# A SwiGLU chunk's silu, gate product and split, emitted in three pieces over three items

## The chip, the cores and the metric

The kernel runs on one core of one Trainium2 chip. The metric is the device time of one execution in microseconds, the lower the better. Engines are named as in the profile: PE (matmuls), PEld (weight loads into PE), DVE (elementwise on tensors), ACT (activations), POOL (small elementwise work and some DMA issues), SP (the queue that issues the weight loads from memory).

## The reference

A trunk of two layers on a sequence of 256 rows and width 1024. Each layer is a half-step SwiGLU, a token mixer (a gated causal mixing beside a sparse attention), and a second half-step SwiGLU. Each has an RMS norm ahead of it and a shift, a scale and a gate that come from a conditioning vector `c` by a matrix `ada_w` per layer.

```python
def swiglu(h, w_in, w_out):
    g, u = jnp.split(h @ w_in, 2, axis=-1)
    return (jax.nn.silu(g) * u) @ w_out

for l in range(DEPTH):
    mod = c_act @ ada_w[l] + ada_b[l]
    sh1, sc1, g1, sh2, sc2, g2, sh3, sc3, g3 = jnp.split(mod, N_MOD, axis=-1)
    h = modulate(rms_norm(x, norm_ffn1[l]), sh1, sc1)
    x = x + 0.5 * g1[:, None, :] * swiglu(h, ffn1_w_in[l], ffn1_w_out[l])
    ...
```

`w_in` is 1024 x 5632 and `w_out` 2816 x 1024, all float32.

## The kernel before

**Three products per product.** Every float32 operand of a matmul is split into a high part (rounded to the fast float32 form) and a low part (the rest). A matmul then is three: high by high, high by low, low by high. So a unit of weights, 512 KB loaded from memory into one of 7 buffers `raw` (`NRAW`), is split before use: ACT copies it to `whi` (L502), DVE subtracts to `wlo` (L507). The pair of `raw` readers, ACT and DVE, frees the buffer, and only then SP issues the next load into it. There are 10 pairs of `whi` and `wlo` (`NB`).

**The conditioning vectors ride along.** Rows of `ada_w` come through the same 7 buffers, woven between the units of weights. DVE multiplies and adds them into `aacc` (L489; the first of eight on ACT, L484). After the eighth, DVE folds the sum (L386), PE multiplies the folded sum by a small matrix (L399 or L431), and DVE finishes it (L402, or L435 and what follows). For the vectors named G the result goes out and back by two small DMAs that POOL issues (L395 fetches `ada_b`, L404 and L406 store and broadcast).

**The phases.** There are six: SwiGLU, mixer and SwiGLU for each layer, numbered 0 to 5. In a SwiGLU phase the 2816 columns are cut into chunks, chunk 0 of 512 columns, chunk 1 of 256, chunks 2 to 5 of 512. In phase 0, chunks 0 and 1 are part of a start-up; in phases 2, 3 and 5 chunk 0 is computed per half of the rows. All others are *joint chunks* (`joint_chunk`): both halves of the rows together, 8 items of one unit of weights each (4 items for chunk 1). A joint chunk takes as many of the 8 PSUM banks as it has blocks of 128 columns, four, or two for chunk 1. A bank holds 256 values of g and 256 of u. An item is 24 matmuls (L719), ordered by bank, so that a chunk's first bank is complete before its last.

After the last item the *gate* of each bank follows: ACT writes silu of g into the scratch tile `xm` (L741), DVE multiplies by u (L742), and the bank is given back. After each pair of banks comes the *split* of the result: ACT writes `aThi` (L536), DVE writes `aTlo` (L537). These are operands of the second product, `project`, which runs over 22 units of `w_out`, first ahead on one half of the rows by up to 7 items (`LAG`), then alternating between halves; an item there is 6 matmuls (L540 to L542).

**What sets the order.** Each engine works through its instructions in the order in which this code emits them, and waits at an instruction until its operands are there. After each item, `item_done` runs what was put off with `defer(n, ...)`, that is n items earlier, and then `pump` emits splits of weights and additions of `ada_w` rows: at most 2 units after an item of a joint chunk, 1 after others, and only while fewer than 8 units lie ahead. In phase 0 the code also emits steps of the rotary tables (`rope_tables`, L163 to L208): POOL does most of them, DVE casts in between (L178, L180, L202), and ACT takes the sines at the end (L198, L200, L206, L208).

Of the kernel before, what the change touches and what calls it, by code (L numbers as in the profile page):

```python
# [25 lines left out]
LAG = 6  # L26
NRAW = 7
HOLD = (3, 7)
TAIL = 3
VX = 188  # L30
FOLD_D = (2, 2, 4)
# [68 lines left out]
def trunk(ctx, tc, x_in, c_in, pos_in, ada_w, ada_b, norm_ffn1, ffn1_w_in, ffn1_w_out,  # L100
# [12 lines left out]
    bankp = ctx.enter_context(tc.tile_pool(name="bankp", bufs=1, space=bass.MemoryType.PSUM))  # L113
    banks = [bankp.tile([P, 512], F32, name=f"bank{i}") for i in range(8)]

    def take():
        return banks.pop(0)

    def give(*ts):
        banks.extend(ts)  # L120
# [206 lines left out]
    def defer(n, fn):  # L327
        pend.append([n, fn])
# [115 lines left out]
    late = []  # L444

    def pump_lo(n=1 << 20):
        while late and n > 0:
            e, hi, lo, r = late.pop(0)
            c = e["kt"] * e["cols"]
            V.tensor_tensor(lo[:, :c], e["raw"][:, :c], hi[:, :c].bitcast(F32), op=ALU.subtract)  # L450
            e["hi"], e["lo"], e["slot"] = hi, lo, r
            W.append(e)
            n_rd[0] += 1
            n -= 1
        dma_fill()
# [61 lines left out]
    def next_w(b):  # L517
        while wcur[b] >= len(W):
            if late:
                pump_lo(1)  # L520
            else:
                pump(1, force=True)
        e = W[wcur[b]]
        wcur[b] += 1
        kt, cols = e["kt"], e["cols"]
        n = kt * cols
        return (e["hi"][:, :n].rearrange("p (k c) -> p k c", k=kt),
                e["lo"][:, :n].rearrange("p (k c) -> p k c", k=kt), e["slot"])

    def release(b, w):  # L530
        if b == 1:
            ring[w[2]] = True


    def split_T(ps, hi, lo):
        S.activation(hi, ps, AF.Copy)  # L536
        V.tensor_tensor(lo, ps, hi.bitcast(F32), op=ALU.subtract)  # L537

    def mm3(ps, ahi, alo, whi, wlo, first, last):
        T.matmul(ps, ahi, whi, start=first, stop=False)  # L540
        T.matmul(ps, ahi, wlo, start=False, stop=False)  # L541
        T.matmul(ps, alo, whi, start=False, stop=last)  # L542
# [54 lines left out]
    def after_sub(b, pi):  # L597
        if pi + 1 < len(phases):
# [3 lines left out]
            pump_lo(1)  # L602
            hold[0] = HOLD[b]

# [22 lines left out]
    def project(b, pi, n, operand, hook):  # L627
        _, l, i, _ = phases[pi]
        final = pi + 1 == len(phases)
        parts = PARTS if final and b == 1 else HALF  # L630
        bk = [take() for _ in parts]
        acc = [t[:, :sl.stop - sl.start] for t, sl in zip(bk, parts)]

        def part(k, w, h):
            ahi, alo = operand(k)
            mm3(acc[h], ahi, alo, w[0][:, 0, parts[h]], w[1][:, 0, parts[h]], k == 0, k == n - 1)
        for k in range(n - TAIL):
            w = next_w(b)
# [4 lines left out]
            yield  # L643
        ws = [next_w(b) for _ in range(TAIL)]
        for h, sl in enumerate(parts):
            for i_ in range(TAIL):
                part(n - TAIL + i_, ws[i_], h)
                if h + 1 == len(parts):
                    release(b, ws[i_])
                if i_ == 1 and h == 0:  # L650
                    hook(n - TAIL)
                    yield
            if h < 2:
                hook(n - TAIL + h + 1)
            if not final and h != b:
# [17 lines left out]
    def ffn_gen(b, pi, env):  # L673
        hi, lo = hT(1, b)
        f = 0
        for c0, w in chunks[:1] if pi else ():
            kt = 1024 // w
            acc = [take() for _ in range(2)]
            for k0 in range(0, KD, kt):
                for s in range(2):  # L680
# [30 lines left out]
    def joint_chunk(env, ch, late=False):  # L711
        c0, w = chunks[ch]
        f, nj = c0 // P, w // P
        acc = [take() for _ in range(nj)]

        def mms(parts, pick):
            for o, col, wk, k, first in parts:
                for i_, (stat, mov) in enumerate(pick):
                    T.matmul(o, wk[stat][col], mov[:, :, k, :], start=first and i_ == 0 and mov is hThi  # L719
                             and stat == 0, stop=False, skip_group_check=True)  # L720

        for k0 in range(0, KD, 2):
            for ss in ((0,), (1,)) if w == 512 else ((0, 1),):
                w_ = next_w(0)
                wcur[1] = wcur[0]
                release(1, w_)
                parts = [(acc[j][:, s * 256:(s + 1) * 256],
                          (slice(None), kk, slice((0 if w == 512 else s * 256) + j * P,
                                                  (0 if w == 512 else s * 256) + j * P + P)),
                          w_, k0 + kk, k0 + kk == 0 and s == ss[0] and s == 0)  # L730
                         for j in range(nj) for kk in range(2) for s in ss]
                if late:
                    for p_ in ((0, hThi), (1, hThi), (0, hTlo)):
                        mms(parts, (p_,))
                else:
                    mms(parts, ((0, hThi), (0, hTlo), (1, hThi)))
                if k0 + 2 == KD and ss[-1] == 1:
                    scr = xm[0] if w == 512 else xm[1]
                    for j in range(nj):
                        a = scr[:, j * 256:(j + 1) * 256]  # L740
                        S.activation(a, acc[j][:, :256], AF.Silu)  # L741
                        V.tensor_tensor(a, a, acc[j][:, 256:], op=ALU.mult)  # L742
                        give(acc[j])
                        if j % 2:
                            def fin(j=j):
                                a2 = scr[:, (j - 1) * 256:(j + 1) * 256].rearrange(
                                    "p (f b t) -> p f b t", f=2, b=2)
                                split_T(a2, env["aThi"][:, f + j - 1:f + j + 1],
                                        env["aTlo"][:, f + j - 1:f + j + 1])
                            if late:  # L750
                                env.setdefault("todo", []).append(fin)
                            else:
                                fin()
                yield

    def joint_gen(env, first):
        for ch in range(first, len(chunks)):
            left = 8 if chunks[ch][1] == 512 else 4
            for _ in joint_chunk(env, ch):
                left -= 1  # L760
                yield left if first == 2 and ch + 1 < len(chunks) else 0
# [432 lines left out]
    def start(env):  # L1194
# [33 lines left out]
        load_cols(1)  # L1228
        load_small()
        ga, gb = joint_chunk(env, 0, True), joint_chunk(env, 1, True)  # L1230
        for g in range(NG):
            more = g + 1 < NG
# [41 lines left out]
    for pi, (kind, l, i, n) in enumerate(phases):  # L1274
        with ExitStack() as es:
            env = {}
# [87 lines left out]
```

## Time and profile before

| what | value |
|---|---|
| median of 3 runs | 996.51 us (995.94 to 996.64) |
| the profiled execution, its own time | 997.6 us |
| its span, first to last instruction | 995.9 us |
| PE busy | 971.5 us, 98% |
| DVE busy | 771.4 us, 77% |
| ACT busy | 531.4 us, 53% |
| POOL busy | 52.3 us, 5% |
| silu L741, 76 instructions | 26.1 us |
| gate product L742, 76 instructions | 29.4 us |
| split on ACT L536 and DVE L537 from `xm`, 38 each | 23.9 us and 26.2 us |
| matmuls L719 of the joint chunks, 3648 | 970.7 us, overlapping |

The time lies 1.7 us above the span, and the profiled execution 1.1 us above the median. Matmuls overlap in the records, so their busy times sum to more than they cover; the rate is read from the distance between starts. Times within the profile count from the span's start.

### The profile page before, as it was taken

To read this page: it belongs to the slowest core of one execution; us is meant where nothing else is said; L and a number is where in the kernel's file an instruction comes from. 1 tells how busy PE (TensorE), PEld (TensorE's weight loads), DVE (VectorE), ACT (ScalarE), POOL (GpSimd) and SP (SyncE) were. 2 spreads that over 40 slices of the span, in tenths; PEclk is the share of its full clock that TensorE was granted. 3 is DMA by queue.
4 is the path that set the end of the run, shared out by engine and by line. 5 is a ranking of instruction groups with operands and counts; after the bars stand their busy time and mean duration, and the time that the engine had idled before them with its cause. 6 is when DMAs were issued, how large, how long until landed. Compare 5 with 4: busy or idle time off the path is not lost.

```text
span 995.9 us, 16619 instructions
## 1 busy us (share of the span) xinstructions
PE 971.5 (98%) x6396; PEld 867.9 (87%) x6396; DVE 771.4 (77%) x1072; ACT 531.4 (53%) x794; POOL 52.3 (5%) x92
## 2 busy tenths in 40 slices
PE   7999997999999999999999999999999999999997
PEld 6899995887787899998888999988878789999886
DVE  6888998778997878886587788866889786766444
ACT  6464554356577755544355455435657776444331
POOL 4012400000000000000000000000000000000000
PEclk9999998999999999999999999999999999999999
DMA  9989998967665589888858888996766556766531
GB/s 334 386 279 335 332 348 342 352 225 239 193 190 151 172 293 336 319 320 311 278 180 297 301 311 304 338 309 183 224 197 191 151 172 215 250 241 231 178 134 43
DMA packets 110416, 253.47 MB, mean 255 GB/s; under 512 B 9138, under 2 KB 27620, under 8 KB 110336
## 3 DMA queue, kind: packets, MB, share of 16 engines
q1 hardware_dynamic: 108256, 248.06, 72.4%
q0 software_dynamic: 1792, 3.82, 1.2%
q8 instruction: 50, 0.82, 0.3%
q10 hardware_dynamic: 288, 0.52, 0.1%
q14 instruction: 30, 0.25, 0.1%
HBM read 251.30 MB, written 1.07 MB: 253 GB/s over the span
## 4 chain that ended last, share of the span: by engine, by line
PE 77%; DVE 13%; DMA 3%; issue 3%; ACT 2%; SPq 0%; POOL 0%; POOLq 0%; DVEq 0%; ACTq 0%
PE bank L719 33%; PE bank L540 14%; PE bank L542 13%; PE bank L541 13%; DVE wlo L507 4%; DVE aacc L489 2%; DMA raw<-in_ffn_w_in_dram 2%; PE bank L805 2%; DMA sraw<-in_ada_w_dram 1%; ACT whi L502 1%; DVE score L900 1%; DVE aacc L1126 1%; DVE sS L948 1%; DVE m L899 1%; DVE nmx L952 1%
## 5 line engine op out<-in xcount | busy, mean ns | idle before, releaser
L502 ACT ACTIVATE whi<-raw 128x1024 fp32r<-128x1024 f32 (+1 forms) x328 | 336.0, 1047 | 264.7 <-PE bank L542 133.5
L507 DVE TENSOR_TENSOR wlo<-raw,whi 128x1024 fp32r<-128x1024 f32 (+1 forms) x313 | 374.1, 1211 | 104.8 <-ACT whi L502 103.5
L719 PE MATMUL bank<-hThi,whi 128*128 128x256 f32 x1216 | 325.7, 279 | 1.8 <-ACT hThi L1164 0.9
L719 PE MATMUL bank<-hThi,wlo 128*128 128x256 f32 x1216 | 322.5, 276 | 0.0
L719 PE MATMUL bank<-hTlo,whi 128*128 128x256 f32 x1216 | 322.5, 276 | 0.0
L719 PEld LDWEIGHTS bank<-hThi,whi 128*128 128x128 f32 x1216 | 223.0, 188 | 4.0 <-ACT hThi L1164 1.5
L719 PEld LDWEIGHTS bank<-hTlo,whi 128*128 128x128 f32 x1216 | 222.2, 188 | 0.1
L719 PEld LDWEIGHTS bank<-hThi,wlo 128*128 128x128 f32 x1216 | 222.1, 188 | 0.0
L540 PE MATMUL bank<-whi,aThi 128*128 128x512 f32 (+1 forms) x374 | 143.2, 383 | 2.3 <-ACT whi L502 2.3
L489 DVE SCALAR_TENSOR_TENSOR aacc<-raw,ccol,aacc 128x1024 f32<-128x1024 f32 x112 | 143.4, 1280 | 0.0
L541 PE MATMUL bank<-wlo,aThi 128*128 128x512 f32 (+1 forms) x374 | 142.4, 381 | 0.8 <-DVE wlo L507 0.8
L542 PE MATMUL bank<-whi,aTlo 128*128 128x512 f32 (+1 forms) x374 | 142.2, 380 | 0.0
L540 PE MATMUL bank<-whi,hThi 128*128 128x512 f32 (+1 forms) x352 | 140.6, 399 | 0.0
L542 PE MATMUL bank<-whi,hTlo 128*128 128x512 f32 (+1 forms) x352 | 135.5, 385 | 0.2 <-DVE hTlo L586 0.2
L541 PE MATMUL bank<-wlo,hThi 128*128 128x512 f32 (+1 forms) x352 | 135.1, 384 | 0.0
L540 PEld LDWEIGHTS bank<-whi,aThi 128*128 128x128 f32 x374 | 71.0, 190 | 16.0 <-ACT whi L502 2.7
L541 PEld LDWEIGHTS bank<-wlo,aThi 128*128 128x128 f32 x374 | 71.1, 190 | 13.8 <-DVE wlo L507 1.1
L542 PEld LDWEIGHTS bank<-whi,aTlo 128*128 128x128 f32 x374 | 71.0, 190 | 13.3
L540 PEld LDWEIGHTS bank<-whi,hThi 128*128 128x128 f32 x352 | 66.3, 188 | 15.3 <-issue 2.0
L542 PEld LDWEIGHTS bank<-whi,hTlo 128*128 128x128 f32 x352 | 66.1, 188 | 15.0 <-DVE hTlo L586 1.1
L541 PEld LDWEIGHTS bank<-wlo,hThi 128*128 128x128 f32 x352 | 66.3, 188 | 11.2
L742 DVE TENSOR_TENSOR xm<-xm,bank 128x256 f32<-128x256 f32 x76 | 29.4, 417 | 38.3 <-ACT xm L741 38.1
(168 smaller groups left out, 679.9 us busy)
## 6 DMA issues: line engine op xcount, KB each, us to landing
raw<-in_ffn_w_in_dram SPq DMA_DIRECT2D x160, 512.0 KB, 5.4
raw<-in_ada_w_dram SPq DMA_DIRECT2D x128, 512.0 KB, 5.7
raw<-in_ffn_w_out_dram SPq DMA_DIRECT2D x88, 512.0 KB, 5.6
raw<-in_mix_w_in_dram SPq DMA_DIRECT2D x40, 512.0 KB, 4.4
sraw<-in_ada_w_dram SPq DMA_DIRECT2D x32, 256.0 KB, 6.0
raw<-in_ffn_w_in_dram SPq DMA_DIRECT2D x32, 256.0 KB, 3.8
raw<-in_mix_w_out_dram SPq DMA_DIRECT2D x16, 512.0 KB, 4.1
vec<-gline POOLq DMA_DIRECT2D x6, 512.0 KB, 5.8
```

The costliest lines, as they stand in the source:

```text
L489: V.scalar_tensor_tensor(aacc, e["raw"], ccol[:, j:j + 1], aacc, op0=ALU.mult, op1=ALU.add)
L502: S.activation(hi[:, :n], src, AF.Copy)
L507: V.tensor_tensor(lo[:, :n], src, hi[:, :n].bitcast(F32), op=ALU.subtract)
L540: T.matmul(ps, ahi, whi, start=first, stop=False)
L541: T.matmul(ps, ahi, wlo, start=False, stop=False)
L542: T.matmul(ps, alo, whi, start=False, stop=last)
L719: T.matmul(o, wk[stat][col], mov[:, :, k, :], start=first and i_ == 0 and mov is hThi and stat == 0, stop=False, skip_group_check=True)
L742: V.tensor_tensor(a, a, acc[j][:, 256:], op=ALU.mult)
L805: T.transpose(ps[:, i * P:(i + 1) * P], src(i), ident)
L899: V.max(out=m8, in_=sc)
L900: V.match_replace(out=sc, in_to_replace=m8, in_values=sc, imm_value=TAKEN)
L948: V.scalar_tensor_tensor(sS[:, e::2, :nk], st["sc"][:, None, :].to_broadcast([P, 2, nk]), -BIG, st["S_ps", g][e][:, :, :nk], op0=ALU.mult, ...
```

## The change

The gates of a joint chunk are no longer emitted as one block after its last item. `gate` is silu and product of one bank, `fin` the split of a pair. In the start-up (`late`) the order stays what it was. In all other joint chunks the first pair of gates is due at the first `item_done` after the chunk's last item (`SPREAD[0]` = 1), the second pair at the second (`SPREAD[1]` = 2), and each pair's split one item after its gates (`SPREAD[2]` = 1). In between, `pump` emits its splits of weights and additions of `ada_w` rows as before. If a bank is asked for and none is free, `take` runs a waiting pair of gates at once. Of 19 such chunks, 16 have two pairs and 3 have one.

```diff
+SPREAD = (1, 2, 1)
...
+    evq = []
+
     def take():
+        while not banks:
+            evq.pop(0)()
         return banks.pop(0)
...
-                    for j in range(nj):
+
+                    def gate(j, scr=scr):
                         a = scr[:, j * 256:(j + 1) * 256]
                         S.activation(a, acc[j][:, :256], AF.Silu)
                         V.tensor_tensor(a, a, acc[j][:, 256:], op=ALU.mult)
                         give(acc[j])
-                        if j % 2:
-                            def fin(j=j):
-                                a2 = scr[:, (j - 1) * 256:(j + 1) * 256].rearrange(
-                                    "p (f b t) -> p f b t", f=2, b=2)
-                                split_T(a2, env["aThi"][:, f + j - 1:f + j + 1],
-                                        env["aTlo"][:, f + j - 1:f + j + 1])
-                            if late:
-                                env.setdefault("todo", []).append(fin)
-                            else:
-                                fin()
+
+                    def fin(j, scr=scr):
+                        a2 = scr[:, (j - 1) * 256:(j + 1) * 256].rearrange(
+                            "p (f b t) -> p f b t", f=2, b=2)
+                        split_T(a2, env["aThi"][:, f + j - 1:f + j + 1],
+                                env["aTlo"][:, f + j - 1:f + j + 1])
+                    for j in range(0, nj, 2):
+                        if late:
+                            gate(j)
+                            gate(j + 1)
+                            env.setdefault("todo", []).append(lambda j=j: fin(j + 1))
+                        else:
+                            def two(j=j, done=[]):
+                                gate(j)
+                                gate(j + 1)
+                                defer(SPREAD[2], lambda: fin(j + 1))
+                            evq.append(two)
+
+                            def due(fn=two):
+                                if fn in evq:
+                                    evq.remove(fn)
+                                    fn()
+                            defer(SPREAD[j // 2], due)
```

The order of instructions on PE, POOL and SP stays the same, up to which PSUM bank a few of them use. On ACT and DVE the gates move against the splits of weights. Lines below 743 carry a number 5 or 6 higher after the change (L502 becomes L507, L742 becomes L748), and those below the changed block 19 higher.

The first place is the end of the last joint chunk of phase 0, chunk 5, on DVE, before the change. `xm` is the scratch tile, `raw` and `whi` a unit of weights or a row of `ada_w`, the bank numbers those of the chunk.

```order
L489 SCALAR_TENSOR_TENSOR aacc<-raw,ccol,aacc 128x1024
L742 TENSOR_TENSOR xm_108<-xm_108,bank_85 128x256
L742 TENSOR_TENSOR xm_108<-xm_108,bank_81 128x256
L537 TENSOR_TENSOR aTlo<-xm_108,aThi 128x512
L742 TENSOR_TENSOR xm_108<-xm_108,bank_87 128x256
L742 TENSOR_TENSOR xm_108<-xm_108,bank_84 128x256
L537 TENSOR_TENSOR aTlo<-xm_108,aThi 128x512
L402 TENSOR_TENSOR aacc<-bank_82,aacc 32x32
L507 TENSOR_TENSOR wlo<-raw,whi 128x1024 x2
L489 SCALAR_TENSOR_TENSOR aacc<-raw,ccol,aacc 128x1024
```

The same place on DVE after the change:

```order
L494 SCALAR_TENSOR_TENSOR aacc<-raw,ccol,aacc 128x1024
L407 TENSOR_TENSOR aacc<-bank_82,aacc 32x32
L748 TENSOR_TENSOR xm_108<-xm_108,bank_85 128x256
L748 TENSOR_TENSOR xm_108<-xm_108,bank_81 128x256
L512 TENSOR_TENSOR wlo<-raw,whi 128x1024
L748 TENSOR_TENSOR xm_108<-xm_108,bank_87 128x256
L748 TENSOR_TENSOR xm_108<-xm_108,bank_84 128x256
L542 TENSOR_TENSOR aTlo<-xm_108,aThi 128x512
L512 TENSOR_TENSOR wlo<-raw,whi 128x1024
L542 TENSOR_TENSOR aTlo<-xm_108,aThi 128x512
L494 SCALAR_TENSOR_TENSOR aacc<-raw,ccol,aacc 128x1024
```

The first split of weights now stands behind two products, where it stood behind four products and two splits; the small sum L402 now stands ahead of the gates; what follows the last row is the same.

The same place on ACT, before the change:

```order
L741 ACTIVATE xm_108<-bank_85 128x256
L741 ACTIVATE xm_108<-bank_81 128x256
L536 ACTIVATE aThi<-xm_108 128x512
L741 ACTIVATE xm_108<-bank_87 128x256
L741 ACTIVATE xm_108<-bank_84 128x256
L536 ACTIVATE aThi<-xm_108 128x512
L502 ACTIVATE whi<-raw 128x1024 x3
```

On ACT after the change:

```order
L747 ACTIVATE xm_108<-bank_85 128x256
L747 ACTIVATE xm_108<-bank_81 128x256
L507 ACTIVATE whi<-raw 128x1024
L747 ACTIVATE xm_108<-bank_87 128x256
L747 ACTIVATE xm_108<-bank_84 128x256
L541 ACTIVATE aThi<-xm_108 128x512
L507 ACTIVATE whi<-raw 128x1024
L541 ACTIVATE aThi<-xm_108 128x512
L507 ACTIVATE whi<-raw 128x1024
```

One copy of weights moved in behind the first two silus, and a second one between the two splits.

The third place is the end of chunk 3 on ACT, where the sines of the rotary tables stand; before:

```order
L741 ACTIVATE xm_108<-bank_84 128x256
L741 ACTIVATE xm_108<-bank_85 128x256
L536 ACTIVATE aThi<-xm_108 128x512
L741 ACTIVATE xm_108<-bank_81 128x256
L741 ACTIVATE xm_108<-bank_87 128x256
L536 ACTIVATE aThi<-xm_108 128x512
L198 ACTIVATE sinT<-ang 128x2x8
L200 ACTIVATE sinT<-ang 128x2x8
L502 ACTIVATE whi<-raw 128x1024 x2
```

After:

```order
L747 ACTIVATE xm_108<-bank_84 128x256
L747 ACTIVATE xm_108<-bank_85 128x256
L203 ACTIVATE sinT<-ang 128x2x8
L205 ACTIVATE sinT<-ang 128x2x8
L507 ACTIVATE whi<-raw 128x1024 x2
L747 ACTIVATE xm_108<-bank_81 128x256
L747 ACTIVATE xm_108<-bank_87 128x256
L541 ACTIVATE aThi<-xm_108 128x512
```

The two sines, which need `ang` from POOL, moved ahead of the second pair of gates and stand directly behind the first.

## Prediction

> **What bounds the kernel now.** I read the page's busy times first, then what PE waits for, then the stretches where it stands still.
>
> ```profile
> span 995.9 us, 16619 instructions
> PE 971.5 (98%) x6396; PEld 867.9 (87%) x6396; DVE 771.4 (77%) x1072; ACT 531.4 (53%) x794; POOL 52.3 (5%) x92
> ```
>
> PE is idle for 995.9 - 971.5 = 24.4 us in all. The change can gain only from these, from a lower clock, or lose. The waits of PE that lie behind a chunk whose gates move:
>
> ```profile
> PE bank L399 <- DVE aacc L386: 3.5, 1, 3.5
> PE bank L540 <- ACT whi L502: 2.3, 1, 2.3
> PE bank L541 <- DVE wlo L507: 0.8, 1, 0.8
> PE bank L719 <- DVE aacc L435: 0.7, 1, 0.7
> ```
>
> The first three sum to 6.6 us and are one place, the start of `project` in phase 0, right behind chunk 5 (columns: start, length, what; the bracket is the idle time ahead):
>
> ```profile
> 161.01 0.39 PE L542 MATMUL bank<-whi,aTlo 128*128 128x512 f32 x1
> 163.69 0.49 PE L540 MATMUL bank<-whi,aThi 128*128 128x512 f32 x1 [2.29 <-ACT whi L502]
> 164.95 0.73 PE L541 MATMUL bank<-wlo,aThi 128*128 128x512 f32 x1 [0.77 <-DVE wlo L507]
> 166.33 0.63 PE L541 MATMUL bank<-wlo,aThi 128*128 128x512 f32 x1
> 166.75 0.63 PE L542 MATMUL bank<-whi,aTlo 128*128 128x512 f32 x1
> 170.89 0.32 PE L399 MATMUL bank<-fold,aacc 128*32 128x32 f32 x2 [3.51 <-DVE aacc L386]
> ```
>
> Since `project` runs 7 items ahead on one half of the rows, PE uses up units faster there than they are split. It lacks a unit at 161.40, gets through it by 167.38, and then stands at L399, the small product of a folded `ada_w` sum, until the fold L386 is done. The clock falls too (by stretch: length, busy time of each engine, then PEclk, DMA share and GB/s):
>
> ```profile
> 161.40:171.14 9.74, 3.18 (x10) 1.80 (x9) 8.85 (x11) 5.59 (x7) 1.06 (x2) 0.69 0.71 251
> 171.14:175.15 4.01, 4.01 (x12) 3.15 (x10) 0.80 (x1) 0.99 (x1) 0.51 (x1) 0.50 1.01 367
> 175.15:200.00 24.85, 24.85 (x111) 20.59 (x110) 19.39 (x17) 9.33 (x10) 1.06 (x2) 1.00 0.93 351
> 350.00:450.00 100.00, 100.00 (x870) 99.38 (x869) 83.83 (x92) 50.75 (x64) 0.55 (x1) 1.00 0.87 320
> ```
>
> At half clock a matmul starts every 0.42 us (166.33 to 166.75), at full clock every 24.85 / 111 = 0.224 us. So half of the 2.43 us from 164.95 to 167.38 and of the 4.01 us to 175.15 is lost: 1.2 + 2.0 = 3.2 us. The place costs **6.6 + 3.2 = 9.8 us**. The last row stands for the later SwiGLU phases: PE runs without a pause at full clock, and no wait in the list above comes from them. There the gates' place can gain nothing.
>
> **Why the splits are late there.** DVE is the slow engine of phase 0. From the gates of chunk 2 to the fold, by groups of instructions (count, busy time and mean, then idle time ahead of them), with the stretch as a whole above:
>
> ```profile
> 86.05:169.59 83.54, 77.54 (x611) 73.47 (x609) 74.96 (x89) 44.27 (x62) 16.21 (x27) 0.97 0.89 336
> L507 DVE TENSOR_TENSOR wlo<-raw,whi 128x1024 fp32r<-128x1024 f32 x30 | 36.2, 1221 | 2.8 <-ACT whi L502 2.6
> L537 DVE TENSOR_TENSOR aTlo<-xm,aThi 128x512 fp32r<-128x512 f32 x8 | 5.5, 693 | 5.6 <-ACT aThi L536 5.6
> ```
>
> DVE is busy 74.96 of 83.54 us. Of its 8.6 us of idle time 5.6 us are eight waits of 0.70 us, two per chunk: it finishes two products, and must wait while ACT writes `aThi`. One such block, and the first split of weights behind each of the other three:
>
> ```profile
> 156.76 0.64 ACT L741 ACTIVATE xm<-bank 128x256 f32<-128x256 f32 x2
> 159.23 0.75 DVE L742 TENSOR_TENSOR xm<-xm,bank 128x256 f32<-128x256 f32 x2
> 162.72 0.69 DVE L537 TENSOR_TENSOR aTlo<-xm,aThi 128x512 fp32r<-128x512 f32 x1 [0.69 <-ACT aThi L536]
> 163.33 0.17 DVE L402 TENSOR_TENSOR aacc<-bank,aacc 32x32 f32<-32x32 f32 x1
> 163.67 2.36 DVE L507 TENSOR_TENSOR wlo<-raw,whi 128x1024 fp32r<-128x1024 f32 x2 [0.17 <-ACT whi L502]
> 169.59 1.25 DVE L386 TRANSPOSE_TENSOR_REDUCE aacc<-aacc 128x32 f32<-128x1024 f32 x1
> 90.50 1.23 DVE L507 TENSOR_TENSOR wlo<-raw,whi 128x1024 fp32r<-128x1024 f32 x1 [0.26 <-ACT whi L502]
> 112.46 1.23 DVE L507 TENSOR_TENSOR wlo<-raw,whi 128x1024 fp32r<-128x1024 f32 x1 [0.47 <-ACT whi L502]
> 134.64 1.23 DVE L507 TENSOR_TENSOR wlo<-raw,whi 128x1024 fp32r<-128x1024 f32 x1 [0.26 <-ACT whi L502]
> ```
>
> While the block runs no `raw` is freed, so SP issues nothing, and memory idles a little later (here behind chunk 3):
>
> ```profile
> 159.34 0.33 SPq L377 DMA_DIRECT2D raw<-in_ada_w_dram  x1
> 164.92 0.33 SPq L368 DMA_DIRECT2D raw<-in_ffn_w_out_dram  x1
> 112.00:116.00 4.00, 4.00 (x38) 4.00 (x37) 3.54 (x4) 4.00 (x5) 0.00 (x0) 1.00 0.39 102
> ```
>
> **The change part by part.** No instruction is added or removed; each of the 76 gates and 38 splits keeps its time.
>
> *The late unit.* ACT takes the unit's copy right behind the first two silus: 156.76 + 0.64 = 157.4, done by 158.5. DVE does L402 (0.17) and two products from 159.23, 0.92 us, then the unit's low part, 1.23 us: 161.4, where it was 164.9. PE needs it at 161.40. Both waits, 2.3 + 0.8, go, even with nothing earlier. What is late next is the fold.
>
> *The fold.* The same DVE work stands ahead of L386 as before, so it comes earlier only by idle time that vanishes. In the new order DVE has a split of weights between the products and `aTlo`, and ACT writes `aThi` beside it. The eight waits go (5.6 us), and the four behind the blocks, 0.26 + 0.47 + 0.26 + 0.17 = 1.2 us: 6.8 us. The other waits on `whi` (2.8 - 1.2 = 1.6 us) are late loads; with the pauses of SP cut up some go, I take 0.8 us, bounds 0 and 1.6.
>
> *The sines.* At chunk 3 ACT now has the sines ahead of two copies of weights. Their input is a chain of 16 POOL instructions that a cast on DVE releases:
>
> ```profile
> 97.44 0.17 DVE L178 CAST ni<-nf 128x16 int32<-128x16 f32 x1
> 97.90 1.22 POOL L183 TENSOR_SCALAR t<-nf 128x16 f32<-128x16 f32 x1 [8.95 <-DVE nf L180]
> 102.64 0.25 POOL L183 TENSOR_SCALAR t<-nf 128x16 f32<-128x16 f32 x1
> 110.10 0.20 POOL L196 TENSOR_SCALAR ang<-ang 128x16 f32<-128x16 f32 x1
> 107.80 0.73 DVE L742 TENSOR_TENSOR xm<-xm,bank 128x256 f32<-128x256 f32 x2
> ```
>
> Before, the sines stood behind the block and waited for nothing. By then DVE has gained 1.7 us at chunk 2 (two waits and 0.26), so the chain ends at 110.3 - 1.7 = 108.6, and DVE is through the first two products at 107.8 - 1.7 + 0.7 = 106.8. ACT passes the sines at 108.9 and finishes its copy at 109.9: DVE waits **3.1 us**. Bounds: 0, if POOL is faster while DVE stands, to 6 us, if all 16 take the 1.2 us of the slow row.
>
> The same operation takes 1.22 and 0.25 us in these rows, the long ones where DVE is dense. The Trainium skill, "SBUF — State Buffer", section "SBUF: two separate sides", says that GpSimd and a DVE instruction with two SBUF inputs hold a shared port pair exclusively, the other blocked. The rows agree, and it speaks against this change: a denser DVE slows this chain.
>
> *Sum at the fold.* 6.8 + 0.8 - 3.1 = 4.5 us: L386 ends at 166.3, not at 170.84, and L399 starts at 166.4, not at 170.89. Bounds: 1.6 us (only chunk 5's own two waits and 0.17 stay gained) to 8.6 us (all idle time).
>
> *The wait of 0.7 us* in chunk 5 is for a bank that L435 reads. DVE is earlier there, so it goes; PE only arrives sooner at L399, so it adds nothing while the fold is what PE waits for.
>
> *The clock.* PE has no pause up to about 162.0 and then one of 4.4 us. Before, with 6.6 us of pauses, it ran slowly from 164.95, and again for 4.0 us after 171.14. I take the loss of that second piece, 2.0 us, bounds 0 and 5.1 (half of the 10.2 us from 164.95 to 175.15): a gain of 3.2 - 2.0 = 1.2 us.
>
> The Trainium skill, "TensorE: Matmul & The Clock Gate", Part 1, has half rate after an idle window of about 3.4 us and full rate after a busy one. The trace agrees: 10.2 us are three windows. By it a pause under 3.4 us might cost nothing, and this one 1.7 to 3.4 us.
>
> *Everything else.* In the 15 joint chunks of phases 2, 3 and 5 the second pair of banks comes free an item later (24 matmuls, 2.7 us). The next chunk takes the four other banks, and these are wanted 8 items later; PE's unbroken 100 us cover it. Without that cover each chunk could lose one split, 1.2 us. After 175 PE again goes without a pause, so what is gained by then stays.
>
> **Sum:** 4.5 + 1.2 = 5.7 us. The profiled execution, 997.6, becomes 991.9. It lies 1.1 us above the median, so I predict 996.5 - 5.7 = **990.8 us**.
>
> **Rivals.**
> - *The fold is in time.* DVE loses nothing to the sines and gains all its idle time: L386 ends at 162.2, as PE arrives. Then the whole 9.8 us and the 0.7 us go: 986.0 us. For it: ACT is 53% busy. Against: the sines.
> - *Only the last block counts.* What was gained before chunk 5 is waited out again for loads, which at 400 GB/s leave DVE little room; L386 gains 1.6 us and the clock 1.2: 993.7 us. For it: the 1.6 us of late loads. Against: memory idles in the pauses of SP, at 0.39 of its share in the row above.
> - *No gain.* The pauses of PE change their place but L386 stays: 995 to 997 us.
> - *Slower: the broadcast meets the loads.* L402 moves ahead of the gates, so the 512 KB of `vec` that follow it, issued at 166.11 in the lull of the loads, now fall among loads at 410 GB/s:
>
> ```profile
> 166.11 0.56 POOL L406 DMA_DIRECT2D vec<-gline  x1 [1.81 <-DVE wlo L507]
> 150.00:160.00 10.00, 10.00 (x47) 8.21 (x46) 9.32 (x10) 4.40 (x6) 0.00 (x0) 1.00 1.02 410
> ```
>
>  512 KB at that rate push the last loads ahead of the fold back by 1.3 us. If loads, not DVE, then set the fold, it comes at 172.1, and if PE, idle from 162.8 in one piece, runs at half clock for the longest bound, it loses 5.1 instead of 3.2: 996.5 + 1.3 + 1.9 = 999.7 us. It decides once the fold is less than 1.9 us earlier. Against it: DVE has only 1.6 us of waits for loads in 83 us.
> - *The change doesn't do what it says.* A gate run early by `take` would change nothing; the rows of the order show the gates of chunks 3 and 5 at their due places. I give it nothing.
>
> **How the numbers follow.** Chances: my sum 0.50 (its own range 988.5 to 993.3), fold in time 0.15, last block 0.17, no gain 0.11, slower 0.07. The range reaches from 985.5, just below the full gain, to 995.5, above the last-block case. A measurement of this kernel can tell about 0.2%, 2 us, from no change; faster than 994.5 are the first two cases and most of the third: 0.80; within 0.13; slower 0.07.
>
> **What would show it.** Right: L540 and L541 wait for nothing at 161; the eight waits of L537 in phase 0 are gone; SP has no pause of 5 us; ACT waits for POOL ahead of `sinT`; L399 starts near 166.4. Wrong: if DVE waits as long for `whi` as it did for `aThi`, or if PE waits in later phases, the sum fails at the fold or at the banks.

## The result and the profile after

The changed kernel takes **990.81 us** (median of five runs, 989.46 to 993.02); the kernel before took 996.51 us (995.31 to 997.88) in runs made beside it. The ratio is 0.9945, with a 95% interval of 0.9934 to 0.9957: 5.5 us faster, between 4.3 and 6.6 (5.7 by the two medians). In a later stretch of runs the same kernel, unedited, took 988.00 us against 996.41 (the last experiments below). The profiled execution took 989.46 us, the fastest of the first five.

The page's first lines, after:

```profile
span 987.7 us, 16607 instructions
PE 969.1 (98%) x6396; PEld 867.1 (88%) x6396; DVE 768.8 (78%) x1072; ACT 530.2 (54%) x794; POOL 56.6 (6%) x92
```

PE is idle for 987.7 - 969.1 = 18.6 us, where it was 24.4. In the list of what PE waits for, one wait of the place behind chunk 5 is left; both waits for the late unit are gone, and so is the one for a bank in chunk 5:

```profile
PE bank L404 <- DVE aacc L391: 2.6, 1, 2.6
```

L404 is the product that stood at L399. It now starts at 163.01, and PE stands still for 2.6 us in one piece. The stretch by pieces (length, busy time of PE, PEld, DVE, ACT, POOL, then PEclk, DMA share, GB/s):

```profile
160.00:164.00 4.00, 1.38 (x6) 0.86 (x5) 3.97 (x4) 1.21 (x2) 0.49 (x1) 0.90 0.90 314
164.00:168.00 4.00, 4.00 (x13) 3.19 (x13) 0.06 (x1) 1.06 (x1) 0.02 (x1) 0.68 1.03 410
168.00:172.00 4.00, 4.00 (x19) 3.30 (x19) 2.94 (x4) 1.15 (x2) 0.51 (x1) 1.00 0.50 161
```

Clock lost after the stop is 4.00 x 0.32 = 1.3 us, and 0.4 more ahead of 164: 1.7 us. From 168 on PE is back at full clock. DVE at the end of chunk 5 (timeline: start, length, what):

```profile
153.18 0.17 DVE L407 TENSOR_TENSOR aacc<-bank,aacc 32x32 f32<-32x32 f32 x1
153.28 0.73 DVE L748 TENSOR_TENSOR xm<-xm,bank 128x256 f32<-128x256 f32 x2
153.94 1.21 DVE L512 TENSOR_TENSOR wlo<-raw,whi 128x1024 fp32r<-128x1024 f32 x1
155.08 0.73 DVE L748 TENSOR_TENSOR xm<-xm,bank 128x256 f32<-128x256 f32 x2
155.74 0.67 DVE L542 TENSOR_TENSOR aTlo<-xm,aThi 128x512 fp32r<-128x512 f32 x1
...
161.71 1.25 DVE L391 TRANSPOSE_TENSOR_REDUCE aacc<-aacc 128x32 f32<-128x1024 f32 x1
```

No row of this stretch has a bracket, those left out included: DVE waits for nothing through the whole block, and most instructions start some 0.07 us before the one ahead ends (153.94 against 153.28 + 0.73 = 154.01).

To compare the fold across executions, its distance from the first fold of the same kind is taken, which lies just ahead of chunk 2's gates; what start-up noise moved drops out. The stretch between the two, for DVE's groups, in the kernel before:

```profile
84.64:169.59 84.95, 78.95 (x623) 74.88 (x621) 76.34 (x92) 44.86 (x65) 16.21 (x27) 0.97 0.89 337
```

And after, with the two groups that held DVE's waits (count, busy time, mean; then idle time):

```profile
83.46:161.70 78.24, 76.92 (x623) 74.19 (x621) 74.73 (x92) 45.46 (x65) 19.02 (x27) 1.00 1.00 376
```

```profile
L512 DVE TENSOR_TENSOR wlo<-raw,whi 128x1024 fp32r<-128x1024 f32 x31 | 37.4, 1219 | 3.5 <-ACT whi L507 3.5
...
L542 DVE TENSOR_TENSOR aTlo<-xm,aThi 128x512 fp32r<-128x512 f32 x8 | 5.4, 678 | 0.0
```

The same 92 instructions take 78.24 us instead of 84.95, **6.7 us less**: idle time falls from 84.95 - 76.34 = 8.6 to 3.5 us, and busy time by 1.6 us. The memory's share rises from 0.89 to 1.00. One pair of executions fixes this only to about 1 us: with phase 0 in the old order the distance is 84.95 us here, 84.8 in e2 and 84.0 in e6 (experiments below), in the new order 78.2 here, 78.3 in e7, 78.4 in e9 and 79.0 in e1. So the fold comes between 5.0 and 6.7 us earlier.

The two profiled executions differ by 995.9 - 987.7 = 8.2 us. It adds up: the first fold came 84.64 - 83.46 = 1.2 us earlier, in front of everything that the change touches; 6.7 us between the folds; and from the second fold to the end 826.31 before and 826.00 after, 0.3 us. But 2.4 of the 8.2 us lie in the choice of executions: the profiled one was 1.1 us above its median before and 1.3 below it after.

### The profile page after: what moved, and what is told of

The parts are those of the page before. It is cut to its first block, busy times and chain, and to the rows that moved or that the text cites. A ratio compares the mean times of both kernels' runs of the same rounds, so it can differ in the third digit from the quotient of the medians.

```text
span 987.7 us, 16607 instructions
## 1 busy us (share of the span) xinstructions
PE 969.1 (98%) x6396; PEld 867.1 (88%) x6396; DVE 768.8 (78%) x1072; ACT 530.2 (54%) x794; POOL 56.6 (6%) x92
## 4 chain that ended last, share of the span: by engine, by line
PE 75%; DVE 13%; DMA 4%; issue 3%; ACT 2%; POOL 1%; SPq 0%; POOLq 0%; DVEq 0%; ACTq 0%
PE bank L724 31%; PE bank L545 14%; PE bank L547 13%; PE bank L546 13%; DVE wlo L512 4%; DVE aacc L494 2%; PE bank L824 2%; DMA raw<-in_ffn_w_in_dram 2%; DMA sraw<-in_ada_w_dram 1%; DVE aacc L1145 1%; ACT sS L978 1%; DVE score L919 1%; ACT whi L507 1%; DMA raw<-in_ffn_w_out_dram 1%; DVE sS L967 1%
## 5 line engine op out<-in xcount | busy, mean ns | idle before, releaser
L507 ACT ACTIVATE whi<-raw 128x1024 fp32r<-128x1024 f32 (+1 forms) x328 | 340.0, 1049 | 268.3 <-PE bank L547 154.9
L747 ACT ACTIVATE xm<-bank 128x256 f32<-128x256 f32 x76 | 26.4, 380 | 62.7 <-PE bank L724 62.7
```

The source lines that it names most:

```text
L507: S.activation(hi[:, :n], src, AF.Copy)
```

## The experiments

Each is timed in five rounds beside the kernel before, whose medians in the three groups were 996.38, 996.62 and 996.41 us. Where a variant keeps the old place for some chunks, these lines run three pieces as one block, under a condition (`pi` is the phase, `ch` the chunk):

```diff
                         if late:
                             ...
+                        elif not (CONDITION):
+                            gate(j)
+                            gate(j + 1)
+                            fin(j + 1)
                         else:
```

### Which phase: e1 and e2

The theory was that phase 0 holds all of the effect. e1 has the change only in phase 0 (`pi == 0`), e2 only in the later phases (`pi > 0`).

> The gates in pieces in phase 0 alone; phases 2, 3 and 5 as before the change. Theory (all of the gain is the stop of PE behind chunk 5 of phase 0): 990.8 us, between 989.5 and 993, like the whole change. Rival (part of it comes from the later phases): above 993.

> The gates in pieces in phases 2, 3 and 5 alone; phase 0 as before the change. Theory: 996.5 us, within 1 us, with the same waits of PE behind chunk 5 (3.5, 2.3 and 0.8 us). Rival (part of the gain or a loss lies in the later phases): below 994.5 or above 998.5.

Measured: e1 **989.21 us**, ratio 0.9928 (0.9913 to 0.9942), a little under the band, with an interval that overlaps the whole change's; e2 **996.23 us**, 0.9998 (0.9990 to 1.0007). PE's waits behind chunk 5 in e2 are those of before, up to 0.2 us:

```profile
PE bank L404 <- DVE aacc L391: 3.4, 1, 3.4
PE bank L545 <- ACT whi L507: 2.3, 1, 2.3
...
PE bank L546 <- DVE wlo L512: 0.8, 1, 0.8
PE bank L724 <- DVE aacc L440: 0.5, 1, 0.5
```

So the gates of the 15 later joint chunks gain and cost nothing that can be measured, and the whole effect is in phase 0.

### Which chunk: e3 and e4

e3 has the change only in phase 0's chunk 5, right ahead of `project` (`pi == 0 and ch == 5`), e4 only in its chunks 2 to 4 (`pi == 0 and ch < 5`).

> The gates in pieces only behind chunk 5 of phase 0. Theory (the fold decides, and idle time of DVE at all four chunks makes it late): the waits at L540 and L541 go, the fold comes only 1.6 us earlier, 993.7 us, between 993 and 995.5, PE waits some 6 us in one piece at the fold's product. Rival (the late unit behind chunk 5 is all of it): 991.

> The gates in pieces behind chunks 2, 3 and 4 of phase 0, chunk 5 and the later phases as before the change. Theory: DVE reaches chunk 5 some 5 us earlier, so the unit is in time for PE although the block at chunk 5 is whole, and the fold is late by chunk 5's own two waits alone, 1.6 us: 992.5 us, between 991 and 994. Rival (the late unit behind chunk 5 is all of it): 996.

Measured: e3 **995.00 us**, 0.9982 (0.9974 to 0.9991); e4 **991.27 us**, 0.9947 (0.9935 to 0.9959). First and last start of the fold in e3, and then in e4 (the fold's row when asked by tile):

```profile
L391 DVE TRANSPOSE_TENSOR_REDUCE aacc<-aacc x4: 1231/1236/1245, 83.0 to 165.8; 128x32 f32<-128x1024 f32 x4
```

```profile
L391 DVE TRANSPOSE_TENSOR_REDUCE aacc<-aacc x4: 1236/1240/1246, 83.4 to 163.7; 128x32 f32<-128x1024 f32 x4
```

The distance is 82.8 us in e3 and 80.3 in e4, against 84.95: 2.1 and 4.7 us less. Together that is 6.8, the 6.7 of the whole change. At the fold the chunks add up, as far as single executions, which differ by up to 1 us, can show it. In e3 neither wait for the late unit is left, but the time moves by only 1.4 us, since the pieces of the stop merge into one:

```profile
PE bank L404 <- DVE aacc L391: 6.4, 1, 6.4
```

The late unit's 3.1 us thus gained little by themselves: PE runs sooner into the product that waits for the fold. What counts is when the fold comes. In e4 neither wait for the late unit is left either, though the block at chunk 5 is whole: PE's only wait there is 3.2 us at L404.

### The same gain without the change: e6

If PE only stands at L399 because its queue is in order, moving that small product three items later in the kernel before should free PE, with the gates where they were.

```diff
-            defer(FOLD_D[2], prod)
+            defer(FOLD_D[2] + (3 if (l, v) == (0, 5) else 0), prod)
```

> The kernel before the change, with PE's product of the second folded sum of phase 0 put three items later. Theory (3.5 us of PE's stop are its place in PE's order, not missing weights): the wait of 3.5 us goes, those of 2.3 and 0.8 stay; with the shorter time at half clock 991.5 us, between 990 and 993.5. Rival (PE then lacks weights instead): 995 or more, with waits at L540 or L541 of 2 us and more behind 167 us.

Measured: **990.54 us**, 0.9945 (0.9931 to 0.9958), as much as the whole change in its first measurement. The waits at that place:

```profile
PE bank L540 <- ACT whi L502: 0.9, 1, 0.9
PE bank L541 <- DVE wlo L507: 0.8, 1, 0.8
PE bank L399 <- DVE aacc L386: 0.4, 1, 0.4
```

The fold itself is nearly where it was (83.5 to 167.5, 84.0 us after the first). The wait of 2.3 us was expected to stay and is 0.9: DVE came 1.0 us earlier here than in the profile before, which the edit does not explain, and PE a little later. Of 6.6 us of waits 2.1 are left, in pieces, and the clock between 158 and 176 is 1.00.

### Both: e7

e7 is the changed kernel with e6's edit.

> The whole change, and PE's product of the second folded sum of phase 0 three items later. Theory: no wait of PE is left behind chunk 5, full clock throughout: 986.5 us, between 985.5 and 988.5. Rival (PE then waits for weights behind it, because DVE waits for the small load of the sum): 990 or more.

Measured: **986.57 us** (986.25 to 986.92), 0.9902 (0.9889 to 0.9915). PE has no wait left behind chunk 5:

```profile
158.00:176.00 18.00, 18.00 (x81) 14.65 (x80) 15.32 (x15) 7.41 (x7) 1.66 (x4) 1.00 0.97 370
```

It beats the kernel before by 10.0 us. All its runs lie below all nine of the changed kernel (987.42 to 993.02), but these were not made beside it, and its interval overlaps that of e9 below. Beside it ran e5 (below), which differs from the changed kernel by an edit that gains nothing: 988.18 us, every run of it above every run of e7. So e7 is faster than the changed kernel too, by some 1.6 us, but this rests on two comparisons.

### The sines: e5 and e8, and once more e9 to e11

The prediction charged the fold with 3.1 us for DVE's wait behind the sines. They wait as told; ACT, after:

```profile
106.83 0.22 ACT L203 ACTIVATE sinT<-ang 128x16 f32<-128x16 f32 x1 [3.95 <-POOL ang L201]
```

and DVE's split of weights behind them waits 2.68 us. e5 emits the sines four steps of the rotary tables later, which is two items, since a joint chunk of phase 0 takes two steps after each item (the "four items" of two expectations below are these four steps). e8 has e5's edit and e7's:

```diff
         G.tensor_scalar(ang, ang, PI_IN, -PI_IN, op0=ALU.min, op1=ALU.max)
         yield
+        for _ in range(4):
+            yield
         S.activation(sinT[:, :, 8:16], ang, AF.Sin)
```

> The whole change, and the two sines emitted two items later, behind the splits of chunk 3. Theory (the wait of ACT for POOL at the sines costs DVE 2.7 us, and these reach the fold): the wait of DVE of 2.7 us behind chunk 3 goes, the fold comes up to 2.6 us earlier, PE waits little or not at all at its product and the clock does not fall: 987 us, between 986 and 989.5. Rival (loads or the gates of chunk 4 take the 2.7 us up again): 990.8.

> The whole change with both the sines and the product of the folded sum later. Theory (either edit alone takes the last wait of PE away): like the product alone, 986.5 us within 1 us. Rival (each has a gain of its own): below 985.

Measured: e5 **988.18 us**, 0.9916 (0.9904 to 0.9929); e8 **986.56 us**, 0.9898 (0.9885 to 0.9911). The time of e5 was what the theory gave, but the trace was not: the fold came only 0.5 us earlier (83.8 to 161.6, 77.8 us). So e5 ran once more beside the changed kernel (e9, unedited), and the edit alone in the kernel before (e11).

> The changed kernel once more, as it is, to have it on the same chip and in the same stretch as the two that follow. Expected: 990.8 us within 1.5, ratio to before 0.9945, with a wait of TensorE's product for the folded ada_w sum behind chunk 5 of 2 to 4 us and half clock behind it.

> The changed kernel with the sines four items later, once more. Theory (the 2.6 us between 990.81 and 988.18 were real: VectorE's fold comes about half a microsecond earlier, the stop of TensorE is then 1.2 us instead of 2.6 and the clock does not fall behind it, worth 1.7): 987 to 989, at least 1.5 us under the copy of the change in the same call, product's wait under 2 us and the clock at 1.00 behind it. Rival (the two kernels differ by chance alone, by where the stop meets the clock's windows and by the start-up): within 1 us of the copy of the change.

> The kernel before with the sines four items later and nothing else. Theory (VectorE's wait for sinT was cover for late loads and for the waits of blocks that follow, so taking it away moves the fold behind chunk 5 by 0.5 us): 995 to 996.5, ratio 0.998 to 1.000, waits of 2.3, 0.8 and about 3 us at the late unit and the product. Rival (the 3.1 us come out at the fold in full, as the prediction had it, and the clock falls less): 992 to 993.5 with a wait for the product of under 1 us.

Measured: e9 **988.00 us**, 0.9914 (0.9901 to 0.9926); e10 **988.46 us**, 0.9917 (0.9903 to 0.9930); e11 **997.71 us**, 1.0013 (1.0005 to 1.0022). Side by side the two kernels do not differ: e5's gain was a difference between stretches of runs, and its theory falls. e9 itself came out 2.8 us under its first measurement, outside what was expected of it. DVE's waits between the folds show why the edit gains nothing; in e9 (timeline, rows with a wait):

```profile
108.19 1.23 DVE L512 TENSOR_TENSOR wlo<-raw,whi 128x1024 fp32r<-128x1024 f32 x1 [2.69 <-ACT whi L507]
146.05 1.23 DVE L512 TENSOR_TENSOR wlo<-raw,whi 128x1024 fp32r<-128x1024 f32 x1 [0.39 <-ACT whi L507]
```

and in e10:

```profile
123.41 1.23 DVE L514 TENSOR_TENSOR wlo<-raw,whi 128x1024 fp32r<-128x1024 f32 x1 [1.40 <-ACT whi L509]
148.79 1.23 DVE L514 TENSOR_TENSOR wlo<-raw,whi 128x1024 fp32r<-128x1024 f32 x1 [1.22 <-ACT whi L509]
```

The 2.69 us are gone, and 1.40 + 1.22 = 2.6 us of waits stand in their place. They have two causes; ACT in e10:

```profile
122.11 0.21 ACT L213 ACTIVATE cosT<-t 128x16 f32<-128x16 f32 x1 [2.49 <-POOL t L211]
122.23 0.20 ACT L215 ACTIVATE cosT<-t 128x16 f32<-128x16 f32 x1
122.33 1.04 ACT L509 ACTIVATE whi<-raw 128x1024 fp32r<-128x1024 f32 x1
...
147.70 1.06 ACT L509 ACTIVATE whi<-raw 128x1024 fp32r<-128x1024 f32 x1 [2.83 <-DMA raw<-in_ffn_w_out_dram]
```

The first, 1.40 us, is the edit's own doing. It moves every later step of the tables too, and now the cosines make ACT wait for POOL ahead of a copy whose load had landed at 119.69. The same wait of 1.4 us stands in e5, e8 and e11, and in neither kernel without the edit. Only the second is a late load, 1.22 us where e9 has 0.39. So e10 exchanges one wait for POOL for another, and what the sines alone cost at the fold it does not tell.

The loads are close behind DVE all the same: in e9 the chain of work that ended last by 175 (starts, lengths) runs through one:

```profile
143.36 6.48 DMA raw<-in_ffn_w_out_dram
149.95 1.07 ACT whi L507
```

e11 came out slower, outside both its theory and its rival. DVE's waits for late copies grew from 2.6 to 4.5 us there, 1.4 of it behind the cosines, and the fold came 1.8 us later (85.1 to 171.9). Its profiled execution is the slowest of its twelve, 1000.66 us.

The stop was shorter and the clock whole in e9; PE's wait, and then the stretches around it:

```profile
PE bank L404 <- DVE aacc L391: 1.6, 1, 1.6
```

```profile
158.00:164.00 6.00, 4.41 (x21) 3.31 (x21) 5.97 (x6) 2.10 (x2) 0.85 (x2) 1.00 0.87 309
164.00:168.00 4.00, 4.00 (x19) 3.30 (x18) 0.26 (x1) 1.19 (x2) 0.22 (x1) 1.00 1.01 387
```

Its fold (83.5 to 161.9) is within 0.2 us of the one in the first profile of the same kernel; PE merely came to its product 1.2 us later (163.21 - 1.59 against 163.01 - 2.62). The spans differ by 987.7 - 986.4 = 1.3 us, about the 1.7 us of clock.

## Why the prediction was right, and where its sizes were not

**990.8 us was forecast and 990.81 measured. The mechanism was right; that the figures meet is luck.** Two terms were off in opposite directions, the fold (4.5 us) too small and the clock (1.2 us) too large, and the same kernel measured 988.00 us later. The steps:

- *Later phases gain nothing:* right, by e2.
- *The late unit:* right. Both waits go, already with chunk 5 alone (e3). As said, the fold is what is late next.
- *The fold, 4.5 us:* too small; 6.7 between the two profiles, 5.0 to 6.7 over all of them. Its own parts held: the eight waits for `aThi` are gone (5.6 us, now 0.0); so are the four behind the blocks but for the one at the sines; waits for late loads fell from 1.6 to 0.6 us, 1.0 where 0.8 was taken. The sines cost 2.7, not 3.1 us. That is 5.6 + 1.2 + 1.0 - 2.7 = 5.1 us of idle time. What was missing is DVE's busy time, forecast as "the same DVE work": it fell by 1.6 us. Instructions that follow each other without a wait overlap in the records by about 0.08 us. Of the 91 steps from one of the 92 instructions to the next, 63 overlap before and 81 after, by 5.2 and 6.6 us in all: 1.4 of the 1.6 us. Shorter instructions (L537 693 to 678 ns, L742 414 to 409) make the other 0.2.
- *The sines as a term of their own:* right in mechanism, and 2.7 us where 3.1 were taken. The fear that a denser DVE slows POOL's chain did not come true: its 16 instructions took 12.0 us (94.82 to 106.80) where they had taken 12.4, and the last ones 0.20 to 0.25 us each, while DVE stood still behind the first two products. The upper bound of 6 us was worked out too low (16 instructions of 1.2 us make 19.2 us instead of 12.4, so 3.1 + 6.8 = 9.9). What the fold would gain without this wait stays open, since e10 has another in its place. The rival in which gains are waited out for loads shows only as the 0.6 us of late loads that are left.
- *The clock, 1.2 us:* this step failed. Its loss after the stop was sized well (2.0 forecast, 1.7 found, none in e9). But of the 3.2 us before, the first 1.2 lay ahead of L399, which waited for the fold anyway, so they had cost nothing; only the 2.0 us behind it could be gained. The term should have read 2.0 - 2.0 = 0. In the profiles it is 0.3 us, and with a whole clock, as in e9, 1.8.
- *The wait of 0.7 us in chunk 5:* right; it goes. PE comes to L404 at 160.4, and in e9 at 161.6. Forecast was a stop of 4.4 us from 162.0; it was 2.6, since the fold came earlier still. L404 started at 163.01, not 166.4: 1.2 of that is start-up noise, 2.2 the fold.
- *SP's pauses:* those of 5 us and more are gone, and behind chunks 2, 4 and 5 none above 2.6 us is left; behind chunk 3 one of 4.2 us stays, where ACT waits for the sines (SP's queue, after):

```profile
104.83 0.34 SPq L382 DMA_DIRECT2D raw<-in_ada_w_dram  x1
109.39 0.37 SPq L373 DMA_DIRECT2D raw<-in_ffn_w_in_dram  x1
```

- *The slower rival*, a broadcast of `vec` that meets the loads: it was issued at 158.35 among loads, as the rival had it, and the fold came 6.7 us earlier all the same:

```profile
158.35 0.56 POOL L411 DMA_DIRECT2D vec<-gline  x1 [4.21 <-DVE aTlo L542]
```

By the corrected terms the change is worth 5.0 to 6.7 us at the fold and 0.3 to 1.8 behind it, 5.3 to 8.5 us. Both measurements, 5.7 and 8.4 us, lie in that. What set the two groups of runs 2.8 us apart is not shown. The mean clock differs: 0.993 to 0.996 in the four runs of the first that were not profiled, 0.997 in the profiled one, 0.996 to 0.999 in e9. Where they lost it no trace shows. A place where clock comes and goes by chance is the start-up: between 8 and 20 us it was 1.00 after the change and 0.86 in e7, ahead of all that e7 edits:

```profile
8.00:20.00 12.00, 8.31 (x55) 6.24 (x55) 9.94 (x17) 9.46 (x16) 6.68 (x19) 1.00 1.09 375
```

```profile
8.00:20.00 12.00, 8.75 (x48) 6.10 (x49) 9.74 (x17) 9.34 (x16) 6.69 (x19) 0.86 1.09 376
```

But it cost e7 little: its first fold came at 83.7 against 83.5 after the change, and its run with this clock took 986.67 us, the other three 986.25 to 986.92. So it need not be what set the first runs apart, and that stays open.

## What to carry to other kernels

Where an engine works in order, ask which single instruction it will stand at next, and whether that one could stand later: one small matmul moved by three items (e6) was worth 6.1 us, spreading the gates of a whole phase 5.7 to 8.4, and both together 10.0 (986.57 against 996.62). Time lost ahead of an instruction that waits anyway, to a low clock or to an engine's own waits, is not to be counted again. An edit that moves one step of a chain moves those behind it too: before its result is read, the trace must show that no new wait stands further on (e10). A few microseconds between two variants count only when they ran side by side: one kernel gave 990.8 and 988.0 us in two groups of runs while the kernel before moved by 0.1.

## What the hardware showed unexpectedly

The length of a stop does not decide alone whether the clock falls. Stops of 2.6 us (after) and 2.3 us (e1) were followed by half clock; those of 1.6 and 1.9 us (e9, e10) and the three pieces of 0.9, 0.8 and 0.4 us (e6) were not. A stop of 2.3 us in e11 was not either. The waits and stretches of e1, where the stop ends at 164.94, and then of e11, where it ends at 165.96 and the next begins at 168.66:

```profile
PE bank L404 <- DVE aacc L391: 2.3, 1, 2.3
164.00:168.00 4.00, 3.06 (x11) 2.50 (x12) 1.99 (x2) 0.90 (x1) 0.51 (x1) 0.80 0.95 326
168.00:172.00 4.00, 4.00 (x15) 3.15 (x14) 0.33 (x2) 0.94 (x2) 0.00 (x0) 0.77 0.97 384
```

```profile
PE bank L542 <- ACT whi L504: 2.3, 1, 2.3
164.00:168.00 4.00, 1.29 (x4) 0.86 (x5) 3.14 (x5) 3.67 (x6) 0.50 (x1) 1.00 0.49 200
```

In the changed kernel the same place costs 1.7 us of clock in one execution (after) and nothing in another (e9).

The Trainium skill, "TensorE: Matmul & The Clock Gate", Part 1, has half rate after an idle window of about 3.4 us, and a window that runs freely, so that it depends on the run where a stop falls in it. The 1.7 us are half of one such window, and the spread from run to run agrees. The 2.6 us of the changed kernel and the 2.3 us of e1 do not fill a window; that they were enough differs from the rule as the page puts it.
